# Who makes the weights' digits: moving casts, subtractions and loads between engines in a one-core layer kernel

## The chip, the core and the metric

The kernel runs on one core of a Trainium2 chip. The core has a matrix engine (TensorE, PE in the profile; its weight loads are PEld), a vector engine (VectorE, DVE), a scalar engine (ScalarE, ACT), a general engine (GpSimd, POOL) and a sync engine (SyncE, SP), which here only issues DMAs. Each engine works through its own instructions in order and waits at semaphores for the others. The metric is the device time of one execution in microseconds (us).

## The reference

One layer of an encoder in fp32, 1024 tokens by 1024 channels:

```python
h = rmsnorm(x, g_mix)
z = h @ w_in                               # pooling channels | q | k | v
y_pool = pool_mixer(z[..., :512], w_pool_grp, pool_scale)
y_attn = diff_attention(q, k, v, ...)      # 8 heads, two softmax maps each, chunk-causal
gates  = sigmoid(h @ w_gate + b_gate)      # 2 x 1024 columns
merged = gates[..., :1024] * (y_pool @ w_branch_pool) \
       + gates[..., 1024:] * (y_attn @ w_branch_attn)
x = x + merged @ w_out
h2 = rmsnorm(x, g_ffn)
x = x + square(relu(h2 @ w_up)) @ w_down
```

## The kernel before

**Digits.** A float32 operand is split into two digits in the matrix engine's fp32r form: hi is the rounded value, lo the rest. A product is three matmuls, hi·hi, hi·lo and lo·hi (`mm3`, L125 to L127). `split` makes the digits: the cast to hi on ACT (L119), the subtraction for lo on DVE, or on POOL where the caller says so (L120).

**Order.** A tile framework schedules the program: it takes instructions in the order in which they become ready in its own model of time, with a priority by program order, and adds the semaphores. `tc.issue_after(i)` lets what stands in the block come no sooner than instruction `i`. So a small edit can move instructions of every engine. After that, each engine's order is fixed.

**Stages** (times of the profile): until some 690 us the eight heads, each over eight tiles of queries: `z` (q, k, v of a tile), ACT's squares and DVE's `ms`, POOL's power (L236), DVE's `qn` (L429), POOL's scaling of `qn` (L435), transposes `tk` (to K and Q), scores `sc`, DVE's maxima `nm` (L490), ACT's exponentials `s` (L498), DVE's difference of the two maps (L507), transposes `ta` (to AT), `po`, and the head's norm (`oq`, `oqs`). Matmuls of the gates and the pooling groups (`g`, `u`, `yp`) fill in between; their weights `fwgate`, `fwpool` are split with lo on POOL, and a gate column half `go` (L733) is stored to `g_dram` by ACT's queue.

Within the heads `weight_unit` also prepares the digits for the attention branch. That branch multiplies by a seven-product scheme on 2 x 2 blocks (products "1" to "7"), so its weights are sums and differences of blocks of `w_branch_attn`. There are eight units. Each loads four blocks (`wq`), makes seven operands with four POOL operations (L767, L779) and calls `put` seven times: `put` splits 128x256 into the tile `wd` and stores it to `wa_dram` by SP (L764). `wd` has two buffers, so a put waits for the store of the one before the last. `PREP_AT` lists the `gate_step`s at which a unit is written.

Then the branches' start (690 to 757 us): `load_split` of the pooling branch's `ypT`, its weights `rbp` and `wbp`, the products `bp`, for each half `gate_half` (a load of `g`, L823, and ACT's sigmoid, L824), and `mp` = `bp` * `g` (L210). `load_a` (L869) issues the loads of the attention branch's digits, `wa`, from `wa_dram`; `y_scaled` and `split_b` make the other operand, `yb`. From 757 to 836 us follow the seven products `baX` and `baY` of 28 steps; behind each product `after(j)` adds it up (`plus`, L925), `gated` multiplies by the gate (L896) and adds `mp` (L897), and `merged` splits the result into `mT`. From 836 us on `op` multiplies `mT` by `w_out`, whose digits `wo` come from `ro` (`load_rows`, L159). Norm and MLP fill the rest.

Of the kernel before, what the change touches and what calls it, by code (L numbers as in the profile page):

```python
# [8 lines left out]
F32 = mybir.dt.float32  # L9
F32R = mybir.dt.float32r  # L10
I32 = mybir.dt.int32
AF = mybir.ActivationFunctionType
ALU = mybir.AluOpType
# [4 lines left out]
P = 128  # L18
S = 1024
# [3 lines left out]
H = 8  # L23
# [13 lines left out]
N_YU = 5  # L37
N_QKVW = 8 * H
N_AHEAD_B, N_AHEAD_A = 5, 3
PREP_AT = (3, 5, 6, 8, 9, 11, 12, 13)  # L40


START = "x0 g n0 w0 w1 w2u w3u x1 s0p s1 x2 s2p s3 x3"
# [14 lines left out]
def encoder_kernel(  # L58
# [21 lines left out]
    nc = tc.nc  # L80
    x, out = x[0], out[0]
    w_in, w_gate, w_out = w_in[0], w_gate[0], w_out[0]
    w_branch_pool, w_branch_attn = w_branch_pool[0], w_branch_attn[0]
# [6 lines left out]
    hp0 = [mix.enter_context(tc.tile_pool(name=f"hp0{i}", bufs=4)) for i in "ab"]  # L90
    hp1 = [mix.enter_context(tc.tile_pool(name=f"hp1{i}", bufs=4)) for i in "ab"]
# [11 lines left out]
    def htile(shape, dt, name, th):  # L103

        hcount[th] += 1
        return (hp1 if th else hp0)[(hcount[th] - 1) // 4 % 2].tile(shape, dt, tag="H", name=name)
# [4 lines left out]
    def raw(shape, name):  # L111
        return rpool.tile(shape, F32, tag="raw", name=name)

    def f(ap):
        return ap.bitcast(F32)

    def split(hi, lo, src, lo_eng=None):

        nc.scalar.copy(hi, src)  # L119
        (lo_eng or nc.vector).tensor_tensor(lo, src, f(hi), op=ALU.subtract)  # L120

    def mm3(ps, lhs_hi, lhs_lo, rhs_hi, rhs_lo, first, last, more=False):

# [15 lines left out]
    def fr_tile(shape, name):  # L139
        return fp.tile(shape, F32, tag="fr", name=name, bufs=N_FR)  # L140
# [15 lines left out]
    def load_rows(src, r0, c0, name, tile_fn):  # L156

        rw = raw([P, 2, 512], f"r{name}")
        nc.sync.dma_start(rw, src[r0 : r0 + 2 * P, c0 : c0 + 512].rearrange("(kk p) c -> p kk c", p=P))  # L159
        ws = []  # L160
        for j in range(2):
            w = tile_fn([P, 2, 512], f"w{name}_{j}")
            split(w[:, 0], w[:, 1], rw[:, j, :], nc.gpsimd)
            ws.append(w)
        return ws

# [17 lines left out]
    def load_split(src, r0, name, tile_fn):  # L184

        rw = raw([P, S], f"r{name}")
        nc.sync.dma_start(rw, src[r0 : r0 + P, :])
        return split_halves(rw, name, tile_fn)

    def y_scaled(d, rbs):  # L190
# [10 lines left out]
    def pair(t):  # L201
        return t[:, 0, :], t[:, 1, :]

    def branch_pool(d, ws, ps_fn):

        m = htile([P, S], F32, f"mp{d}", 1)
        gs_ = [gate_half(d, th) for th in range(2)]
        for th in range(2):
            ps = proj_T(ps_fn(f"bp{d}_{th}"), ws, lambda k, th: pair(ypT[k][th]), th, nk=4)
            nc.vector.tensor_tensor(m[:, th * 512 : (th + 1) * 512], ps, gs_[th], op=ALU.mult)  # L210
        mp.append(m)


    identf = units.tile([P, P], F32, name="identf")
# [9 lines left out]
    cols = const.tile([P, 24], F32, name="cols")  # L224
# [5 lines left out]
    g_dram = dram.tile([2 * D, S], F32, name="g_dram")  # L230
# [45 lines left out]
    with ExitStack() as ph:  # L276
# [356 lines left out]
        for g in range(-2, N + 8):  # L633
# [11 lines left out]
            for tok in ORDER:  # L645
                if tok not in gens:
                    i = g - tok[1]
# [7 lines left out]
    def fill_w(src, c0, name):  # L655
        ws = []
        for j in range(2):
            rw = fr_tile([P, 4, P], f"fr{name}_{j}")
            nc.sync.dma_start(
                rw, src[j * 512 : (j + 1) * 512, c0 : c0 + P].rearrange("(kk p) c -> p kk c", p=P)  # L660
            )
            w = fw_tile([P, 2, 4, P], f"fw{name}_{j}")
            split(w[:, 0], w[:, 1], rw, nc.gpsimd)
            ws.append(w)
        return ws

# [61 lines left out]
    def gate_cols(c):  # L728
        ws = fill_w(w_gate, c * P, f"gate{c}")
        for th in range(2):  # L730
            ps = fill_proj(ws, th, f"g{c}_{th}", spare_bank if c >= G_Z else fill_bank)
            fo = fo_tile(f"go{c}_{th}")
            stored["go"] = nc.scalar.activation(fo[:, 0:512], ps, AF.Identity, bias=cols[:, c : c + 1]).ins  # L733
            nc.scalar.dma_start(g_dram[c * P : (c + 1) * P, th * 512 : (th + 1) * 512], fo[:, 0:512])
            yield

# [5 lines left out]
            yield  # L742

    stored = {}
    wa_dram = dram.tile([28, P, 2, 512], F32, name="wa_dram")
    ORDER_BA = [(j, kk) for j in "1267543" for kk in range(4)]

    def weight_unit(src, digits, kk, ch):

        cs = slice(ch * 256, (ch + 1) * 256)  # L750
        q = fq.tile([P, 4, 256], F32, tag="mx", name=f"wq{kk}_{ch}")
        for i in range(2):
            r0 = (kk + 4 * i) * P
            nc.sync.dma_start(
                q[:, i::2, :], src[r0 : r0 + P, :].rearrange("p (i c) -> p i c", i=2)[:, :, cs]
            )
        a11, a12, a21, a22 = (q[:, i, :] for i in range(4))
        buf = fu_tile(f"wd{kk}_{ch}").rearrange("p (s h c) -> p s h c", s=2, h=2)

        def put(j, a):  # L760
            d = buf[:, nput[0] % 2]
            nput[0] += 1
            split(d[:, 0, :].bitcast(F32R), d[:, 1, :].bitcast(F32R), a, nc.gpsimd)
            nc.sync.dma_start(digits[ORDER_BA.index((j, kk))][:, :, cs], d)  # L764

        def minus(o, x_, y_):
            nc.gpsimd.tensor_tensor(o, x_, y_, op=ALU.subtract)  # L767

        nput = [0]
        put("1", a11)  # L770
        minus(a21, a11, a21)
        put("7", a21)
        put("2", a12)
        minus(a21, a22, a21)
        put("6", a21)
        put("4", a22)
        minus(a12, a12, a21)
        put("3", a12)
        nc.gpsimd.tensor_tensor(a11, a11, a21, op=ALU.add)  # L779
        put("5", a11)  # L780
# [3 lines left out]
    units_left = [(kk, ch) for kk in range(4) for ch in range(2)]  # L784

    def gate_step():
        more = next(gate_units, "end") != "end"
        steps[0] += 1
        if steps[0] in PREP_AT:
            with tc.issue_after(stored["go"]):  # L790
                weight_unit(w_branch_attn, wa_dram, *units_left.pop(0))
        return more

    for _ in range(G_FIRST):
        gate_step()
    for g in range(4):
        for _ in pool_group(g):
            gate_step()
    while gate_step():
        pass  # L800
    assert not units_left
# [18 lines left out]

    def gate_half(r0, th):
        gt = tmp(f"g{r0}_{th}")
        nc.sync.dma_start(gt, g_dram[r0 * P : (r0 + 1) * P, th * 512 : (th + 1) * 512])  # L823
        nc.scalar.activation(gt, gt, AF.Sigmoid, bias=zero)  # L824
        return gt

# [1 line left out]
        return [fu_tile(f"rb{d}")] if d in (0, 1, 2, 3, 5) else [tmp(f"rb{d}_{i}") for i in range(2)]  # L828

    ws_bp = {0: load_cols2(w_branch_pool, 0, "bp0", wt)}  # L830
    yr, wr, mp, mT = {}, {}, [], {}
    for d in range(NK - 2):
        yr[d] = y_scaled(d, row_factors(d))
    ypT = [load_split(p_dram, g * P, f"ypT{g}", ypt_tile) for g in range(4)]
# [31 lines left out]
    def load_a(n):  # L866

        wa_ba[n] = wa = (ut([P, 2, 512], F32R, f"wa{n}") if n < 8 or n > 23 else fw_tile([P, 2, 512], f"wa{n}"))
        nc.sync.dma_start(f(wa), wa_dram[n])  # L869
# [24 lines left out]
    def gated(d, th, c, src=None):  # L894

        nc.vector.tensor_tensor(c, src or c, gate_half(NK + d, th), op=ALU.mult)  # L896
        nc.gpsimd.tensor_tensor(c, c, mp[d][:, th * 512 : (th + 1) * 512], op=ALU.add)  # L897

    def merged(d, th, c):

        mT[d, th] = t = (hp1 if th else hp0)[d // 4].tile([P, 2, 512], F32R, tag="H", name=f"mT{d}_{th}")
        split(t[:, 0, :], t[:, 1, :], c)

    for d in range(NK):
        if d % 2 == 0 and d + 2 < NK:
            ws_bp[d + 2] = load_cols2(w_branch_pool, (d + 2) * P, f"bp{d + 2}", fw_tile)
        branch_pool(d, ws_bp[d - d % 2][d % 2], bank)
        if d == 1:
            for k in (6, 7):
                yr[k] = y_scaled(k, row_factors(k))  # L910
        load_a(d)
        if d > 2:
            split_b(d - 3)
    Yb = [bank(f"baY{dd}") for dd in range(4)]
    Xb = [bank(f"baX{dd}") for dd in range(4)]
    kept_ba = {}
# [11 lines left out]
    def after(j):  # L928

        if j == "1":  # L930
            copies("x1", Xb, [h_slab(f"x1_{i}") for i in range(2)])
        elif j == "2":
            for dd, c in plus("x1", Yb):
                gated(dd, 0, c)
                merged(dd, 0, c)
        elif j == "6":
            copies("U2", Xb, [up_slab(f"bU2_{i}") for i in range(2)])
        elif j == "7":
            copies("z7", Yb, [h_slab(f"z7_{i}") for i in range(2)])
        elif j == "5":  # L940
            for dd, c in plus("z7", Xb):
                gated(4 + dd, 1, c)
        elif j == "4":
            for dd, c in plus("U2", Yb):
                gated(4 + dd, 0, c)
                merged(4 + dd, 1, kept_ba["z7"][dd])
                merged(4 + dd, 0, c)
        else:
            for dd, c in enumerate(slabs([up_slab(f"c12_{i}") for i in range(2)])):
                gated(dd, 1, c, Xb[dd])  # L950
                merged(dd, 1, c)
# [492 lines left out]
```

## Time and profile before

| | |
|---|---|
| median of 3 runs | 1561.0 us (1560.26 to 1564.82) |
| the profiled execution | 1558.39 us, with a span of 1556.6 us |
| PE / DVE / ACT / POOL busy | 98% / 68% / 53% / 26% of the span |
| TensorE clock granted, mean | 0.999 |
| DMA | 235.81 MB, mean 151 GB/s |

All times of instructions come from one profiled execution. A row of a view names line, engine, operation and tiles (out<-in), with times in us and the mean of one instruction in ns; a row of waits names the engine and line that sat idle, and behind the arrow what released it. L12 is line 12 of the kernel before.

### The profile page before, as it was taken

The page shows a single profiled execution, that of the slowest core. Times are in us where ns is not written, and L with a number is a line of the kernel's source. Part 1 is how long each engine was busy: PE and PEld are TensorE (multiplying, and loading weights), DVE is VectorE, ACT ScalarE, POOL GpSimd, SP SyncE. Part 2 cuts the span into 40 slices and gives each one's busy share as a digit, 9 for nine tenths or more (in the row PEclk, how much of TensorE's full clock was granted, in tenths as well). Part 3 has the DMA queues.
Part 4 walks back from the last instruction along what each step waited for, and adds up shares of the span by engine and source line. Part 5 has one row for each costly group of instructions (what it writes and reads, how often), then busy time and mean ns, then how long its engine had stood idle before and what let it go on. Part 6 is the DMA issues. An engine that isn't in the chain of part 4 may idle for free.

```text
span 1556.6 us, 22409 instructions
## 1 busy us (share of the span) xinstructions
PE 1521.2 (98%) x7601; PEld 1310.7 (84%) x7601; DVE 1055.0 (68%) x2309; ACT 832.5 (53%) x1864; POOL 400.2 (26%) x520
## 2 busy tenths in 40 slices
PE   7999999999999999999999998999999999999999
PEld 6998988889998999877887887888888788888887
DVE  7777666687878787765569448776666568646662
ACT  6666566565656565554344556565555634333331
POOL 6446767451526252312037400000000000000000
PEclk9999999999999999999999999999999999999999
DMA  7133444220202021446576733545442689637750
GB/s 242 57 110 111 144 134 158 97 84 28 84 28 77 31 90 44 174 159 236 169 269 196 227 111 114 178 165 185 137 143 108 236 312 391 209 122 236 240 193 27
DMA packets 183277, 235.81 MB, mean 151 GB/s; under 512 B 11685, under 2 KB 114810, under 8 KB 183162
## 3 DMA queue, kind: packets, MB, share of 16 engines
q1 hardware_dynamic: 165754, 207.08, 40.0%
q10 hardware_dynamic: 17408, 27.30, 4.7%
q8 instruction: 60, 0.98, 0.3%
q14 instruction: 55, 0.45, 0.1%
HBM read 165.10 MB, written 69.24 MB: 151 GB/s over the span
## 4 chain that ended last, share of the span: by engine, by line
PE 47%; DMA 2%; DVE 2%; issue 2%; ACT 1%; POOL 1%; SPq 0%; POOLq 0%; ACTq 0%; DVEq 0%
PE Da L125 4%; PE Da L127 4%; PE Da L126 4%; PE Db L125 3%; PE Db L127 3%; PE Db L126 3%; PE X L125 2%; PE X L127 2%; PE X L126 2%; PE Z L127 2%; PE Z L126 2%; PE Z L125 2%; PE op L127 2%; PE op L125 1%; PE op L126 1%
## 5 line engine op out<-in xcount | busy, mean ns | idle before, releaser
L125 PE MATMUL z<-wqkv,hT 128*128 128x384 f32 x512 | 174.3, 340 | 1.4 <-DVE qn L429 1.4
L126 PE MATMUL z<-wqkv,hT 128*128 128x384 f32 x512 | 173.4, 339 | 0.5 <-POOL wqkv L120 0.5
L127 PE MATMUL z<-wqkv,hT 128*128 128x384 f32 x512 | 173.3, 339 | 0.0
L498 ACT ACTIVATE s<-s,nm 128x256 f32<-128x256 f32 (+7 forms) x128 | 99.6, 779 | 62.8 <-DVE nm L490 59.7
L125 PE MATMUL g<-hT,fwgate 128*128 128x512 f32 x256 | 101.0, 394 | 0.2 <-ACT go L733 0.2
L125 PEld LDWEIGHTS z<-wqkv,hT 128*128 128x128 f32 x512 | 96.5, 188 | 5.0 <-DVE qn L429 2.1
L127 PE MATMUL g<-hT,fwgate 128*128 128x512 f32 x256 | 100.7, 394 | 0.0
L126 PE MATMUL g<-hT,fwgate 128*128 128x512 f32 x256 | 100.6, 393 | 0.0
L126 PEld LDWEIGHTS z<-wqkv,hT 128*128 128x128 f32 x512 | 96.5, 188 | 4.0 <-POOL wqkv L120 1.0
L127 PEld LDWEIGHTS z<-wqkv,hT 128*128 128x128 f32 x512 | 96.4, 188 | 2.4 <-DVE hT L120 0.5
L236 POOL TENSOR_TENSOR ms<-ms,mhalf 128x4 f32<-128x4 f32 x64 | 67.1, 1049 | 102.5 <-DVE ms L235 86.0
L490 DVE CUSTOM_DVE_ANT_0 s<-sc,dist 128x512 f32<-128x512 f32 (+3 forms) x128 | 74.9, 586 | 11.9 <-PE sc L488 10.1
L120 POOL TENSOR_TENSOR wqkv<-rqkv,wqkv 128x384 fp32r<-128x384 f32 x60 | 63.8, 1082 | 22.2 <-ACT wqkv L119 19.0
L120 DVE TENSOR_TENSOR AS<-s,AS 128x512 fp32r<-128x512 f32 x64 | 43.8, 689 | 37.9 <-ACT AS L119 37.8
L487 PE MATMUL sc<-K,Q 128*128 128x512 f32 (+2 forms) x192 | 66.6, 358 | 0.5 <-DVE nm L490 0.4
L488 PE MATMUL sc<-K,Q 128*128 128x512 f32 (+2 forms) x192 | 65.9, 357 | 0.0
L458 ACT CAST Q<-tk 64x128 fp32r<-64x128 f32 x128 | 33.0, 258 | 51.2 <-DVE K L457 50.1
L457 DVE TENSOR_TENSOR K<-tk,K 64x128 fp32r<-64x128 f32 x128 | 37.0, 289 | 34.2 <-ACT K L456 31.0
L435 POOL TENSOR_TENSOR qn<-qn,ggh 128x128 f32<-128x128 f32 x64 | 32.2, 503 | 101.5 <-DVE qn L429 93.8
L461 ACT CAST Q<-tk 64x128 fp32r<-64x128 f32 x128 | 33.2, 260 | 42.3 <-DVE Q L460 40.7
L125 PEld LDWEIGHTS g<-hT,fwgate 128*128 128x128 f32 x256 | 48.1, 188 | 8.4 <-ACT go L733 0.5
L127 PEld LDWEIGHTS g<-hT,fwgate 128*128 128x128 f32 x256 | 48.1, 188 | 8.3
(460 smaller groups left out, 4740.9 us busy)
## 6 DMA issues: line engine op xcount, KB each, us to landing
wd<-in_w_down_dram SPq DMA_DIRECT2D x56, 512.0 KB, 5.4
wu<-in_w_up_dram SPq DMA_DIRECT2D x32, 512.0 KB, 4.5
udS<-us SPq DMA_DIRECT2D x64, 256.0 KB, 2.5
ur<-udS SPq DMA_DIRECT2D x32, 512.0 KB, 3.3
wa_dram<-wd SPq DMA_DIRECT2D x56, 256.0 KB, 2.4
wa<-wa_dram SPq DMA_DIRECT2D x28, 512.0 KB, 6.0
rqkv<-in_w_in_dram SPq DMA_DIRECT2D x64, 192.0 KB, 2.7
ud<-u ACTq DMA_DIRECT2D x48, 256.0 KB, 2.3
```

Of the source, the lines that this page charges most:

```text
L120: (lo_eng or nc.vector).tensor_tensor(lo, src, f(hi), op=ALU.subtract)
L125: nc.tensor.matmul(ps, lhs_hi, rhs_hi, start=first, stop=False, **kw)
L126: nc.tensor.matmul(ps, lhs_hi, rhs_lo, start=False, stop=False, **kw)
L127: nc.tensor.matmul(ps, lhs_lo, rhs_hi, start=False, stop=last, **kw)
L236: nc.gpsimd.tensor_tensor(dst, dst, mhalf[:, :n], op=ALU.pow)
L457: nc.vector.tensor_tensor(K[other, m, c0 : c0 + P], k, f(k_hi), op=ALU.subtract)
L458: nc.scalar.copy(q_hi, q)
L461: nc.scalar.copy(Q[other, m, 1, :], q)
L487: nc.tensor.matmul(dst, Q[:, i, 0, :], rhs, start=True, stop=False)
L488: nc.tensor.matmul(dst, Q[:, i, 1, :], rhs, start=False, stop=True)
L490: nc.vector.tensor_tensor_reduce(out=s[i][:, c : c + w], in0=sc[:, 0:w], in1=dist[:, o0 + c : o0 + c + w], scale=2.0 ** -(h + 1), scalar=B ...
L498: nc.scalar.activation(s[i][:, 0:n], s[i][:, 0:n], AF.Exp, bias=last, scale=-1.0, accum_out=Z[:, i, t : t + 1])
```

## The change

Five things change.

1. `put` takes the cast to hi from ACT to POOL (L762 of the changed kernel); lo stays on POOL (L763).
2. `PREP_AT` has five steps in place of eight, and the other three units are written after the pooling groups 0, 1 and 2. A unit is ordered behind the last lo subtraction of `fwgate` or `fwpool`, no longer behind the last `go`.
3. `load_a(d)` is ordered behind the load of a gate half: that of `g0` for d below 4, that of `g` d − 1 from there on.
4. `mp` is no tile of 1024 columns any more but two halves, in pool tiles of hp1 that two neighbouring d share; `z7` is turned into `mT` at product "5" and not at "4".
5. The gated add (L897 before, L904 after) and the lo subtractions of `wo` are on DVE, no longer on POOL.

```diff
-PREP_AT = (3, 5, 6, 8, 9, 11, 12, 13)
+PREP_AT = (3, 5, 7, 9, 12)
...
-            split(w[:, 0], w[:, 1], rw[:, j, :], nc.gpsimd)
+            split(w[:, 0], w[:, 1], rw[:, j, :])
...
-        m = htile([P, S], F32, f"mp{d}", 1)
...
-            nc.vector.tensor_tensor(m[:, th * 512 : (th + 1) * 512], ps, gs_[th], op=ALU.mult)
-        mp.append(m)
+            nc.vector.tensor_tensor(mp[d, th], ps, gs_[th], op=ALU.mult)
...
-            split(w[:, 0], w[:, 1], rw, nc.gpsimd)
+            stored["lo"] = split(w[:, 0], w[:, 1], rw, nc.gpsimd).ins
...
-            stored["go"] = nc.scalar.activation(fo[:, 0:512], ps, AF.Identity, bias=cols[:, c : c + 1]).ins
+            nc.scalar.activation(fo[:, 0:512], ps, AF.Identity, bias=cols[:, c : c + 1])
...
-            split(d[:, 0, :].bitcast(F32R), d[:, 1, :].bitcast(F32R), a, nc.gpsimd)
+            nc.gpsimd.tensor_copy(d[:, 0, :].bitcast(F32R), a)
+            nc.gpsimd.tensor_tensor(d[:, 1, :].bitcast(F32R), a, d[:, 0, :], op=ALU.subtract)
...
         if steps[0] in PREP_AT:
-            with tc.issue_after(stored["go"]):
-                weight_unit(w_branch_attn, wa_dram, *units_left.pop(0))
+            prepare_weights()
         return more
+
+    def prepare_weights():
+        with tc.issue_after(stored["lo"]):
+            weight_unit(w_branch_attn, wa_dram, *units_left.pop(0))
...
         for _ in pool_group(g):
             gate_step()
+        if g < 3:
+            prepare_weights()
...
-        nc.gpsimd.tensor_tensor(c, c, mp[d][:, th * 512 : (th + 1) * 512], op=ALU.add)
+        nc.vector.tensor_tensor(c, c, mp[d, th], op=ALU.add)
...
+    for i, (a_, th) in enumerate(((0, 0), (2, 0), (4, 1), (6, 1), (4, 0), (6, 0), (0, 1), (2, 1))):
+        t = hp1[i // 4].tile([P, 2, 512], F32, tag="H", name=f"mp{a_}_{th}")
+        mp[a_, th], mp[a_ + 1, th] = t[:, 0, :], t[:, 1, :]
...
-        load_a(d)
+        with tc.issue_after(loaded["g0_1" if d < 4 else f"g{d - 1}_1"]):
+            load_a(d)
...
             for dd, c in plus("z7", Xb):
                 gated(4 + dd, 1, c)
+                merged(4 + dd, 1, c)
         elif j == "4":
             for dd, c in plus("U2", Yb):
                 gated(4 + dd, 0, c)
-                merged(4 + dd, 1, kept_ba["z7"][dd])
                 merged(4 + dd, 0, c)
```

Three places show how the instructions' order moves. The first is POOL in the second head. `ms` and `qn` belong to the query tiles, `wd` and `wq` to a weight unit. Before:

```order
L236 TENSOR_TENSOR ms_4_1541<-ms_4_1541,mhalf 128x4
L120 TENSOR_TENSOR wd_1_7339<-wq_1_7336,wd_1_7339 128x256 x2
L767 TENSOR_TENSOR wq_1_7336<-wq_1_7336 128x256
L779 TENSOR_TENSOR wq_1_7336<-wq_1_7336 128x256
L120 TENSOR_TENSOR wd_1_7339<-wq_1_7336,wd_1_7339 128x256 x2
L767 TENSOR_TENSOR wq_1_7336<-wq_1_7336 128x256
```

In the changed kernel the same engine, in the first head (L234 and L433 there are L236 and L435 here, L762 is the cast, L763 the subtraction):

```order
L762 CAST wd_0_7244<-wq_0_7241 128x256
L234 TENSOR_TENSOR ms_4_719<-ms_4_719,mhalf 128x4
L762 CAST wd_0_7244<-wq_0_7241 128x256
L763 TENSOR_TENSOR wd_0_7244<-wq_0_7241,wd_0_7244 128x256
L433 TENSOR_TENSOR qn_3_651<-qn_3_651,ggh_364 128x128
L120 TENSOR_TENSOR fwgate_0_7300<-frgate_0_7298,fwgate_0_7300 128x512
L763 TENSOR_TENSOR wd_0_7244<-wq_0_7241,wd_0_7244 128x256
L767 TENSOR_TENSOR wq_0_7241<-wq_0_7241 128x256
L762 CAST wd_0_7244<-wq_0_7241 128x256
```

Two operations for each put now stand in POOL's queue between the `ms` and `qn` of the tiles, and the units begin a head earlier; in order, five of them stand in the first part of the heads and three in later heads.

The second place is SP's queue at the branches' start, where `g` is a gate half, `wa` a step's digits, `rypT` and `rbp` the pooling branch's operands. Before:

```order
L823 DMA g_0_8978<-g_dram 128x512
L869 DMA wa_8975<-wa_dram 128x1024
L869 DMA wa_9028<-wa_dram 128x1024
L869 DMA wa_9073<-wa_dram 128x1024
L823 DMA g_1_8981<-g_dram 128x512
L869 DMA wa_9110<-wa_dram 128x1024
L187 DMA rypT_8916<-p_dram 128x1024
L187 DMA rypT_8924<-p_dram 128x1024
L869 DMA wa_9158<-wa_dram 128x1024
L148 DMA rbp_8932<-in_w_branch_pool_dram 128x4x256
```

The changed kernel's SP queue from the same load on (L828 is the gate half there, L876 the digits):

```order
L828 DMA g_0_8984<-g_dram 128x512
L828 DMA g_1_8987<-g_dram 128x512
L187 DMA rypT_8916<-p_dram 128x1024
L187 DMA rypT_8924<-p_dram 128x1024
L148 DMA rbp_8940<-in_w_branch_pool_dram 128x4x256
L148 DMA rbp_9036<-in_w_branch_pool_dram 128x4x256
L828 DMA g_0_8948<-g_dram 128x512
L148 DMA rbp_9119<-in_w_branch_pool_dram 128x4x256
L159 DMA ro_0_9945<-in_w_out_dram 128x2x512
L828 DMA g_1_8951<-g_dram 128x512
L876 DMA wa_8982<-wa_dram 128x1024
```

The first load of `wa` now stands behind two gate halves of each of the first columns, the pooling branch's operands and a load of `w_out`.

The third place is DVE at the end of the products, where `bU` holds half the merged result, `c` the last quarter, and `mT` takes the split. Before:

```order
L120 TENSOR_TENSOR mT_0_9794<-bU_0_9545,mT_0_9794 128x512
L120 TENSOR_TENSOR mT_1_9802<-z_0_9619,mT_1_9802 128x512
L120 TENSOR_TENSOR mT_0_9805<-bU_0_9545,mT_0_9805 128x512
L120 TENSOR_TENSOR mT_1_9813<-z_1_9620,mT_1_9813 128x512
L896 TENSOR_TENSOR c_0_9880<-baX_9292,g_1_9882 128x512
L120 TENSOR_TENSOR mT_0_9816<-bU_1_9546,mT_0_9816 128x512
```

The changed kernel's DVE there (L903 is the gate's product, L904 the add that was POOL's, `wo` a split of `w_out`):

```order
L904 TENSOR_TENSOR bU_0_9545<-bU_0_9545,mp_0_8936 128x512 x2
L904 TENSOR_TENSOR bU_1_9546<-bU_1_9546,mp_0_8937 128x512 x2
L903 TENSOR_TENSOR c_0_9880<-baX_9292,g_1_9882 128x512
L120 TENSOR_TENSOR wo_6_0_10103<-ro_6_10101,wo_6_0_10103 128x512
L120 TENSOR_TENSOR wo_6_1_10106<-ro_6_10101,wo_6_1_10106 128x512
L903 TENSOR_TENSOR c_0_9880<-baX_9293,g_1_9890 128x512
L120 TENSOR_TENSOR mT_0_9803<-bU_0_9545,mT_0_9803 128x512
```

The adds and two subtractions of `wo` now stand ahead of the first `mT` from `bU`, and the splits of `z` have moved up, out of this stretch. On PE the first `op` tile that needs this `mT` (`op_0_9979` with `wo_4`) comes after 12 matmuls before, and after 19 in the changed kernel, since a second token tile's matmuls stand in between.

More of the change, by code (lines that the diff above doesn't have):

```diff
@@ L119, in split @@
         nc.scalar.copy(hi, src)
-        (lo_eng or nc.vector).tensor_tensor(lo, src, f(hi), op=ALU.subtract)
+        return (lo_eng or nc.vector).tensor_tensor(lo, src, f(hi), op=ALU.subtract)
     def mm3(ps, lhs_hi, lhs_lo, rhs_hi, rhs_lo, first, last, more=False):
@@ L186, in load_split @@
         rw = raw([P, S], f"r{name}")
-        nc.sync.dma_start(rw, src[r0 : r0 + P, :])
+        loaded[name] = nc.sync.dma_start(rw, src[r0 : r0 + P, :]).ins
         return split_halves(rw, name, tile_fn)
@@ L744, in encoder_kernel @@
     stored = {}
+    loaded = {}
     wa_dram = dram.tile([28, P, 2, 512], F32, name="wa_dram")
@@ L822, in gate_half @@
         gt = tmp(f"g{r0}_{th}")
-        nc.sync.dma_start(gt, g_dram[r0 * P : (r0 + 1) * P, th * 512 : (th + 1) * 512])
+        loaded[f"g{r0}_{th}"] = nc.sync.dma_start(
+            gt, g_dram[r0 * P : (r0 + 1) * P, th * 512 : (th + 1) * 512]
+        ).ins
         nc.scalar.activation(gt, gt, AF.Sigmoid, bias=zero)
@@ L830, in encoder_kernel @@
     ws_bp = {0: load_cols2(w_branch_pool, 0, "bp0", wt)}
-    yr, wr, mp, mT = {}, {}, [], {}
+    yr, mp, mT = {}, {}, {}
     for d in range(NK - 2):
@@ L896, in gated @@
         nc.vector.tensor_tensor(c, src or c, gate_half(NK + d, th), op=ALU.mult)
-        nc.gpsimd.tensor_tensor(c, c, mp[d][:, th * 512 : (th + 1) * 512], op=ALU.add)
+        nc.vector.tensor_tensor(c, c, mp[d, th], op=ALU.add)
     def merged(d, th, c):
-        mT[d, th] = t = (hp1 if th else hp0)[d // 4].tile([P, 2, 512], F32R, tag="H", name=f"mT{d}_{th}")
+        mT[d, th] = t = (hp1[1 - d // 4] if th else hp0[d // 4]).tile([P, 2, 512], F32R, tag="H", name=f"mT{d}_{th}")
         split(t[:, 0, :], t[:, 1, :], c)
+    for i, (a_, th) in enumerate(((0, 0), (2, 0), (4, 1), (6, 1), (4, 0), (6, 0), (0, 1), (2, 1))):
+        t = hp1[i // 4].tile([P, 2, 512], F32, tag="H", name=f"mp{a_}_{th}")
+        mp[a_, th], mp[a_ + 1, th] = t[:, 0, :], t[:, 1, :]
     for d in range(NK):
```

## The prediction

> **What bounds the kernel now.** I read the page's totals first, then what TensorE waits for, then the busy time by stretch.
>
> ```profile
> span 1556.6 us, 22409 instructions
> PE 1521.2 (98%) x7601; PEld 1310.7 (84%) x7601; DVE 1055.0 (68%) x2309; ACT 832.5 (53%) x1864; POOL 400.2 (26%) x520
> ```
>
> TensorE (PE) is busy 98% of the span. The change leaves its matmuls as they are, so it can win only from the remaining 1556.6 − 1521.2 = 35.4 us, and can lose without a limit. Next comes the list of what PE waited for (total, times, longest).
>
> ```profile
> PE hps L262 <- DVE hn L257: 9.5, 2, 8.7
> PE ta L543 <- DVE s L507: 2.7, 1, 2.7
> PE op L127 <- DVE mT L120: 1.7, 2, 0.9
> PE bp L125 <- DVE mp L210: 1.5, 1, 1.5
> PE z L125 <- DVE qn L429: 1.4, 2, 1.0
> PE tk L447 <- ACT Q L461: 1.2, 1, 1.2
> PE po L579 <- DVE oqs L120: 0.9, 1, 0.9
> PE u L125 <- ACT go L733: 0.7, 1, 0.7
> PE po L126 <- DVE AT_4l L120: 0.5, 1, 0.5
> PE op L125 <- ACT mT L119: 0.5, 1, 0.5
> PE z L126 <- POOL wqkv L120: 0.5, 1, 0.5
> PE sc L487 <- DVE nm L490: 0.4, 1, 0.4
> ```
>
> The first row is the start, which the change does not touch. I sort the others by stage. In the heads, ACT or DVE was late in ta 2.7, tk 1.2, u 0.7 and sc 0.4, together 5.0 us; POOL stands behind z 1.4 (qn needs ms from POOL) and z 0.5, together 1.9. At the branch start there are bp 1.5, oqs 0.9 and AT_4l 0.5, together 2.9. At the merge there are op 1.7 and 0.5, together 2.2. All that the change can reach is therefore 12.0 us.
>
> Busy time by stretch (columns: stretch, its length, PE, PEld, DVE, ACT, POOL, then clock, DMA share, GB/s) shows how much room the other engines have:
>
> ```profile
> 100.00:200.00 100.00, 99.50 (x581) 91.57 (x579) 70.39 (x227) 62.71 (x184) 57.45 (x78) 1.00 0.35 114
> 200.00:300.00 100.00, 94.92 (x547) 85.81 (x545) 67.82 (x223) 62.95 (x186) 63.15 (x87) 1.00 0.43 138
> 300.00:400.00 100.00, 97.75 (x564) 89.76 (x563) 79.24 (x254) 64.15 (x191) 41.62 (x59) 1.00 0.18 56
> 780.00:840.00 60.00, 60.00 (x265) 49.13 (x264) 46.89 (x50) 33.33 (x58) 35.07 (x23) 1.00 0.70 237
> 840.00:920.00 80.00, 77.87 (x361) 63.81 (x360) 41.16 (x60) 32.96 (x62) 28.22 (x24) 1.00 0.62 201
> ```
>
> **Part 1, digits by POOL and spread.** The tile wd tells what the 56 puts cost, and who waited for whom:
>
> ```profile
> L119 ACT CAST wd<-wq x56: 391/407/428, 81.4 to 300.7; 128x256 fp32r<-128x256 f32 x56
> L120 POOL TENSOR_TENSOR wd<-wq,wd x56: 723/739/1255, 81.9 to 301.2; 128x256 fp32r<-128x256 f32 x56
>   ACT wd L119: 30.8, 20
>   DMA wa_dram<-wd: 28.1, 25
> ```
>
> ACT waited 28.1 us for a store to free the double buffer, with softmax work of the heads queued behind it; POOL waited 30.8 us for ACT's cast. One such wait can be followed on ACT at the stall of tk:
>
> ```profile
> 273.66 0.40 ACT L119 CAST wd<-wq 128x256 fp32r<-128x256 f32 x1 [1.07 <-DMA wa_dram<-wd]
> 273.97 0.26 ACT L461 CAST Q<-tk 64x128 fp32r<-64x128 f32 x1
> ```
>
> The cast of Q (L461), for which tk waited 1.2 us, stood behind a cast of wd that waited 1.07 us for a store. After the change both the casts and this wait leave ACT: 56 × 0.407 = 22.8 us of work and 28.1 of waiting. I credit the whole 5.0 us that ACT and DVE lost in the heads (from 0, if other work is the cause, to 5.0): that is 5.0/28.1 = 0.18 us of PE per us of wait.
>
> POOL takes 56 casts of 128x256. No row shows this cast on POOL; the nearest are these:
>
> ```profile
> L767 POOL TENSOR_TENSOR wq<-wq 128x256 f32<-128x256 f32 x24 | 19.3, 803 | 18.4 <-DMA wq<-in_w_branch_attn_dram 18.0
> L706 POOL COPY sum<-u 128x1 f32<-128x1 f32 x8 | 2.2, 280 | 3.7 <-ACT u L698 2.3 <-DMA g_dram<-go 1.3
> wa_dram<-wd SPq DMA_DIRECT2D x56, 256.0 KB, 2.4
> ```
>
> The floor is 0.28 us (a copy of one column), the top 0.80 (a subtraction of the same tile). I take 0.76, the mean of the wd subtraction (42.0 us by 56 is 0.75; same tile, same output form): 56 × 0.76 = 42.6 us, between 15.7 and 45. The Trainium skill ("GPSIMD Engine Reference", 4.1 Engine selection) calls an elementwise op of one input roughly line-rate on GpSimd and a two-input one about twice as slow; a cast by that estimate would be near 0.4 us and the casts near 23, which no row here shows, and my sum goes by the 42.6.
>
> What does it do to the queue behind it? POOL's ms (L236) and qn (L435) are passed on to DVE and so to z and tk. Over the 222 us of wd, POOL was busy about 0.60 and blocked by ACT's cast for 30.8/222 = 0.14, so occupied for 0.74. After the change this block is gone, the casts add 42.6/222 = 0.19 to 0.60, and the store wait comes to POOL. The store takes 2.4 us and a put on POOL 0.76 + 0.75 = 1.5, with other POOL work in between; I estimate half of the 28.1, 14 us or 0.06. That makes 0.85. Units 1 to 5 stay in the first 230 us by the order, so I take this dense case; three later units go to stretches where POOL has 58 of 100 us free. Waits grow like r/(1 − r), from 2.85 to 5.7, so the 1.9 us of POOL's lateness doubles: +1.9 (0 if spread work stays hidden; if nothing is hidden, (42.6 + 28.1) × 0.18 = +12.7). Heads: −5.0 + 1.9 = **−3.1**.
>
> A rule that speaks against it stands beside these rows, DVE's scaled subtractions in the heads:
>
> ```profile
> L507 DVE SCALAR_TENSOR_TENSOR s<-s,cf,s x32: 870/1152/1725, 84.5 to 696.6; 128x640 f32<-128x640 f32 x8, 128x768 f32<-128x768 f32 x8, 128x896 f32<-128x896 f32 x8, 128x1024 f32<-128x1024 f32 x8
> L120 DVE TENSOR_TENSOR oqs<-oq,oqs 128x256 fp32r<-128x256 f32 x32 | 18.2, 570 | 6.4 <-ACT oqs L119 5.8
> ```
>
> By the Trainium skill ("SBUF — State Buffer", section "SBUF: two separate sides"), a GpSimd operation that reads SBUF and a DVE operation with two SBUF inputs lock each other out for a whole instruction. The spread of 870 to 1725 ns over these shapes neither shows nor excludes it. By that rule casts would hold up (32 × 1.15 + 18.2)/700 = 8% of DVE's time against 42.6 us, 3.4 us on DVE, some 0.6 on PE: 1555 in place of my time. My sum leaves it out.
>
> **Parts 3 and 4, the branch start.** The chain of waits runs here through a gate column's store and its load, before sigmoid and product mp. The rows behind it give what such transfers usually take, what SP issued, and the first product:
>
> ```profile
> 710.87 7.68 DMA g_dram<-go
> 718.57 3.60 DMA g<-g_dram
> g_dram<-go ACTq DMA_DIRECT2D x32, 256.0 KB, 2.5
> wa<-wa_dram SPq DMA_DIRECT2D x28, 512.0 KB, 6.0
> 709.94 1.41 SPq L869 DMA_DIRECT2D wa<-wa_dram  x3
> L125 PE MATMUL baX<-yb,wa x64: 387/389/499, 759.3 to 835.4; 128*128 128x512 f32 x64
> ```
>
> The store took 7.68 us where 2.5 is usual, and three loads of wa had been issued on SP 0.9 us before it. With load_a behind the gate loads, these wa loads leave SP's queue here and this store meets less traffic: bp's 1.5 goes, and of the other 1.4 I take 0.5 (AT and oqs belong to the last head's tail on ACT and DVE). **−2.0**, between −2.9 and +6.0, one landing of a wa load, if the first product then waits for it; that product starts at 759.3, 37 us after this load of g lands, so I take no loss. The two-half mp tiles and the earlier mT of z7 issue the same operations: nothing.
>
> **Part 5, the merge.** POOL gives up 24 subtractions of wo and 16 gated adds; DVE takes 40 operations of 128x512 with two SBUF inputs. Prices:
>
> ```profile
> L897 POOL TENSOR_TENSOR bU<-bU,mp x4: 1739/1741/1748, 827.3 to 837.5; 128x512 f32<-128x512 f32 x4
> 836.31 1.77 DVE L120 TENSOR_TENSOR mT<-bU,mT 128x512 fp32r<-128x512 f32 x1
> L120 DVE TENSOR_TENSOR AS<-s,AS 128x512 fp32r<-128x512 f32 x64 | 43.8, 689 | 37.9 <-ACT AS L119 37.8
> ```
>
> DVE pays 0.69 us for such a subtraction where POOL has nothing to do, and 1.77 for the same size while POOL works: 40 × 0.69 = 27.5 us more work between 780 and 920, where DVE was busy 46.89 + 41.16 of 140. It fits in the 52 us free, and the stretched ones shrink besides. An add of 1.74 on POOL becomes 0.69 on DVE in the chain bU, mT, op; PE meanwhile does 19 op matmuls on mT 0 to 3 before the first on mT 4. So the 1.7 us of op behind DVE goes; the 0.5 behind ACT's mT stays: **−1.7**, between −2.2 and +1.5. The loss would come from wo's last subtractions, which now stand in DVE's queue ahead of mT and wait for their load of ro.
>
> **Sum.** −3.1 − 2.0 − 1.7 = −6.8. The profiled execution took 1558.4 us, of which the span is 1556.6; it becomes 1551.6. The median of the runs shown, 1561.0, is 2.6 above it; so 1554.2, said as 1554.
>
> **Rivals.** *Slower, by the store wait on POOL.* Every put waits 2.4 − 1.5 = 0.9 us for its buffer, 56 × 0.9 = 50 us, with ms and qn queued behind it, and POOL's 42.6 + 50 = 93 us cost PE the same 0.18 each: +16.7. With −5.0, −2.0 and −1.7 that is +8.0: 1569. It decides from POOL's cost of 5.0 + 3.7 + 4.7 = 13.4 us on (74 us of lateness). For it: POOL's 63.15 of 100. Against it: wgate and ms work between the puts gives the store time.
>
> *Same, the wait only changes engine.* What ACT gives, POOL takes: heads 0, and −3.7 remains: 1557.3. For it: the heads' chain goes round through all engines, DVE at 70 to 79 of 100 among them.
>
> *More: every listed wait goes,* −12.0: 1549.0. For it: POOL no longer waits for ACT at all. Against it: ends of waits are seldom given back whole, the next engine in the heads' chain is late instead.
>
> **How the numbers follow.** About 0.3% (4.7 us) is what a measurement of this kernel can tell from no change: faster is below 1556.3, slower above 1565.7. Forecast 0.48, same 0.27, more 0.12, slower 0.13. From the forecast's spread (heads −5 to 0) some 0.04 falls in "same". So faster 0.56, same 0.31, slower 0.13. The range reaches from the rival that gains more to the edge of the slower one, 1548 to 1565; the forecast's own is 1551 to 1558.
>
> **What the profile after would show.** Right: no wait for the store on ACT, casts of wd on POOL near 0.76 us or below; rows ta, tk and u gone from PE's waits; the go store near 710 at 2.5 to 4 us, bp's row gone; mT on DVE near 0.69 and op's row under 0.5. Wrong: new rows z behind qn or tk behind POOL of more than 5 us between 50 and 230, POOL at 90 of 100 there; baX waiting for wa at 760; op waiting for mT behind ro.

## The result, and the profile after

The changed kernel takes 1556.0 us (median of 9 runs, 1551.5 to 1558.3) against 1560.3 for the kernel before: a ratio of 0.9966, with a 95% interval of 0.9953 to 0.9979, some 5 us less. The profiled execution is the quickest of the nine, 1551.45 us with a granted clock of 1.000; in the other eight the clock was 0.996 to 0.999 and the span 1552 to 1557 us. Its span is 7.1 us shorter than that of before, so about 2 us of this belong to the execution and not to the change. I read places from the traces, and sizes from the ratios.

The page's totals after:

```profile
span 1549.5 us, 22331 instructions
PE 1519.3 (98%) x7601; PEld 1309.8 (85%) x7601; DVE 1052.1 (68%) x2349; ACT 814.5 (53%) x1808; POOL 361.0 (23%) x536
```

POOL does less than before, although it took 56 casts over: it gave away 40 longer operations. What PE waited for (total, times, longest):

```profile
PE hps L260 <- DVE hn L255: 8.8, 1, 8.8
PE ta L541 <- DVE AT_4l L120: 2.0, 2, 1.6
PE X L125 <- ACT U L1213: 2.0, 1, 2.0
PE sc L485 <- DVE nm L488: 1.9, 4, 0.7
PE Z L125 <- ACT BT1h L119: 1.5, 1, 1.5
PE ta L541 <- DVE ms L233: 1.4, 1, 1.4
PE ta L541 <- ACT Q L459: 1.2, 1, 1.2
...
PE z L125 <- DVE qn L427: 0.7, 1, 0.7
```

The rows of bp, po and op are gone. In the heads ta no longer waits for `s`, nor u for `go`, but others of the same size came: ta behind AT_4l, `ms` and Q, and sc behind `nm` grew from 0.4 to 1.9 us. Busy time by stretch says when (columns as before: PE, PEld, DVE, ACT, POOL, clock, DMA share, GB/s):

```profile
100.00:200.00 100.00, 99.91 (x586) 92.50 (x585) 75.91 (x249) 59.89 (x174) 57.65 (x87) 1.00 0.32 104
200.00:300.00 100.00, 99.69 (x590) 92.51 (x589) 71.42 (x241) 59.91 (x179) 42.01 (x64) 1.00 0.20 67
400.00:500.00 100.00, 96.26 (x555) 87.42 (x554) 76.44 (x250) 59.48 (x174) 49.73 (x76) 1.00 0.24 79
600.00:700.00 100.00, 96.75 (x512) 82.57 (x511) 65.32 (x182) 50.35 (x134) 25.45 (x34) 1.00 0.37 126
700.00:780.00 80.00, 80.00 (x355) 66.12 (x355) 38.20 (x61) 33.97 (x56) 9.80 (x8) 1.00 0.68 232
840.00:920.00 80.00, 80.00 (x378) 66.38 (x378) 43.81 (x74) 34.40 (x66) 3.80 (x7) 1.00 0.60 198
```

Between 200 and 300 us PE's idle time fell from 5.1 us to 0.3; between 400 and 700 it grew. Over the whole heads nothing was won. The same view for the first 700 us in one row, first of before, then of after:

```profile
0.00:700.00 700.00, 679.54 (x3869) 617.85 (x3870) 519.21 (x1614) 432.14 (x1237) 324.50 (x464) 1.00 0.32 103
```

```profile
0.00:700.00 700.00, 679.04 (x3871) 616.13 (x3872) 519.33 (x1623) 412.79 (x1182) 345.27 (x520) 1.00 0.31 99
```

Idle 20.5 us before, 21.0 after. The branch start (700 to 780) went from 2.3 to 0, the end of the merge (840 to 920) from 2.1 to 0. These 4.4 us make up most of what the changed kernel won: PE's idle time over the whole span fell from 35.4 to 30.2 us. The question is what became of the heads' gain.

### The profile page after: what moved, and what is told of

It reads as the page before. It is cut to its first block, busy times and chain, and to the rows that moved or that the text cites. A ratio compares the mean times of both kernels' runs of the same rounds, so it can differ in the third digit from the quotient of the medians.

```text
span 1549.5 us, 22331 instructions
## 1 busy us (share of the span) xinstructions
PE 1519.3 (98%) x7601; PEld 1309.8 (85%) x7601; DVE 1052.1 (68%) x2349; ACT 814.5 (53%) x1808; POOL 361.0 (23%) x536
## 4 chain that ended last, share of the span: by engine, by line
PE 84%; DVE 6%; DMA 3%; issue 3%; ACT 2%; SPq 1%; POOL 0%; POOLq 0%; ACTq 0%; DVEq 0%
PE z L125 5%; PE z L127 5%; PE z L126 5%; PE Da L126 4%; PE Da L127 4%; PE Da L125 4%; PE g L125 3%; PE g L126 3%; PE g L127 3%; PE Db L126 3%; PE Db L127 3%; PE Db L125 3%; PE X L125 2%; PE X L127 2%; PE X L126 2%
## 5 line engine op out<-in xcount | busy, mean ns | idle before, releaser
L234 POOL TENSOR_TENSOR ms<-ms,mhalf 128x4 f32<-128x4 f32 x64 | 67.0, 1046 | 96.2 <-DVE ms L233 79.4
L488 DVE CUSTOM_DVE_ANT_0 s<-sc,dist 128x512 f32<-128x512 f32 (+3 forms) x128 | 74.6, 584 | 17.6 <-PE sc L486 16.1
L120 DVE TENSOR_TENSOR AS<-s,AS 128x512 fp32r<-128x512 f32 x64 | 43.8, 687 | 35.5 <-ACT AS L119 35.3
L120 POOL TENSOR_TENSOR fwgate<-frgate,fwgate 128x512 fp32r<-128x512 f32 x32 | 43.4, 1361 | 87.4 <-ACT fwgate L119 78.8
L125 PEld LDWEIGHTS g<-hT,fwgate 128*128 128x128 f32 x256 | 48.1, 188 | 9.9 <-ACT go L731 1.1
L127 PEld LDWEIGHTS g<-hT,fwgate 128*128 128x128 f32 x256 | 48.0, 188 | 8.7
L126 PEld LDWEIGHTS g<-hT,fwgate 128*128 128x128 f32 x256 | 48.1, 188 | 8.0
```

The lines of the kernel that those rows point to most:

```text
L120: return (lo_eng or nc.vector).tensor_tensor(lo, src, f(hi), op=ALU.subtract)
L125: nc.tensor.matmul(ps, lhs_hi, rhs_hi, start=first, stop=False, **kw)
L126: nc.tensor.matmul(ps, lhs_hi, rhs_lo, start=False, stop=False, **kw)
L127: nc.tensor.matmul(ps, lhs_lo, rhs_hi, start=False, stop=last, **kw)
L234: nc.gpsimd.tensor_tensor(dst, dst, mhalf[:, :n], op=ALU.pow)
L488: nc.vector.tensor_tensor_reduce(out=s[i][:, c : c + w], in0=sc[:, 0:w], in1=dist[:, o0 + c : o0 + c + w], scale=2.0 ** -(h + 1), scalar=B ...
```

## The experiments

All ratios are against the kernel before, run on the same chip. "Idle" is PE's idle time in a stretch, its length less PE's busy time.

| run | 0 to 700 | 700 to 780 | 780 to 920 | ratio (95%) |
|---|---|---|---|---|
| before | 20.5 | 2.3 | 2.1 | 1 |
| changed kernel | 21.0 | 0 | 0 | 0.9966 (0.9953 to 0.9979) |
| part 1 alone | 15.0 | 0.9 | 2.4 | 0.9966 (0.9953 to 0.9979) |
| part 5 alone | 19.5 | 1.0 | 0.3 | 0.9977 (0.9967 to 0.9987) |
| parts 1 and 5 | 15.5 | 1.7 | 0 | 0.9927 (0.9913 to 0.9942) |
| changed, without 3 | 20.9 | 0 | 0 | 0.9982 (0.9971 to 0.9994) |
| changed, without 5 | 21.4 | 0 | 4.6 | 1.0021 (1.0009 to 1.0033) |
| changed, without 1 | 24.2 | 1.2 | 0 | 1.0044 (1.0028 to 1.0059) |
| changed, without 2 | 16.2 | 1.5 | 0 | 0.9916 (0.9902 to 0.9930) |
| changed, without 2 and 3 | 16.9 | 2.0 | 0 | 0.9929 (0.9917 to 0.9941) |
| one late unit | 18.0 | 2.3 | 0 | 0.9969 (0.9957 to 0.9981) |
| late units, no POOL work | 19.4 | 0.4 | 0 | 0.9963 (0.9950 to 0.9975) |
| late units, four copies | 13.8 | 0 | 0 | 0.9908 (0.9886 to 0.9930) |

**Part 1 alone**, in the kernel before:

```diff
-            split(d[:, 0, :].bitcast(F32R), d[:, 1, :].bitcast(F32R), a, nc.gpsimd)
+            nc.gpsimd.tensor_copy(d[:, 0, :].bitcast(F32R), a)
+            nc.gpsimd.tensor_tensor(d[:, 1, :].bitcast(F32R), a, d[:, 0, :], op=ALU.subtract)
```

> The kernel before with part 1 alone: POOL makes the hi digits of wd, the units stay where they were (82 to 301 us in the trace of before). Theory A (the trace of after: PE's idle time in the first 700 us was 20.5 us before and 21.0 after, so the heads gave nothing): taking the casts off ACT removes the idle time between 100 and 300 us (5.6 us before), and new waits of ta, sc or tk come up elsewhere in the heads; the span changes by less than 2 us, ratio 0.999 to 1.001. Theory B (the prediction's): the 5.0 us of the heads are won and POOL gives back 1.9: -3 us, ratio 0.998. Rival C (the store wait on POOL holds up ms and qn): z and tk wait over 5 us more, +8 us, ratio 1.005. In all of them a cast of 128x256 on POOL takes about 0.40 us, as after.

Theory A fell: the heads' idle time went down by 5.4 us and stayed down. B was nearer, with one difference: POOL gave nothing back. The row of the first 700 us, and the tile wd with what its engine waited for:

```profile
0.00:700.00 700.00, 684.96 (x3906) 625.77 (x3907) 527.05 (x1624) 420.01 (x1188) 344.14 (x520) 1.00 0.33 106
```

```profile
L763 POOL CAST wd<-wq x56: 389/397/933, 43.6 to 264.0; 128x256 fp32r<-128x256 f32 x56
L764 POOL TENSOR_TENSOR wd<-wq,wd x56: 728/738/1569, 44.7 to 265.9; 128x256 fp32r<-128x256 f32 x56
...
  DMA wa_dram<-wd: 8.7, 9
```

A cast takes 397 ns, and POOL waits 8.7 us for stores where ACT had waited 28.1. A few waits of PE under 1.5 us are left in the heads (g, sc, ta, trr); none is behind qn. The one behind POOL, trr for the head's norm (1.4 us, after 600 us), comes more than 330 us after the last cast. The merge keeps its 2.4 us, since part 5 is not in it.

**Part 5 alone**, in the kernel before: the subtractions of wo and the gated adds on DVE.

```diff
-            split(w[:, 0], w[:, 1], rw[:, j, :], nc.gpsimd)
+            split(w[:, 0], w[:, 1], rw[:, j, :])
...
-        nc.gpsimd.tensor_tensor(c, c, mp[d][:, th * 512 : (th + 1) * 512], op=ALU.add)
+        nc.vector.tensor_tensor(c, c, mp[d][:, th * 512 : (th + 1) * 512], op=ALU.add)
```

> The kernel before with part 5 alone: gated adds and wo's subtractions on DVE, mp still a tile of 1024 columns and z7 merged at product 4. Theory A (the merge won 2.1 us by DVE no longer being stretched beside POOL): PE's idle time in 840 to 920 us falls from 2.1 to under 0.6, DVE's subtraction mT from bU goes from 1.63 to 0.69 us, span -1.5 to -2.1, ratio about 0.999. Rival D (it was the earlier mT of z7, part 4, that won it): op still waits 1 us or more for mT, ratio 1.000.

Theory A held, D fell: without the earlier mT of z7 the wait of op is gone as well. The gain by the ratio, 0.0023 or 3.6 us, is more than the 0.001 that A named.

**The changed kernel without part 5**, the same edit the other way round:

```diff
-            split(w[:, 0], w[:, 1], rw[:, j, :])
+            split(w[:, 0], w[:, 1], rw[:, j, :], nc.gpsimd)
...
-        nc.vector.tensor_tensor(c, c, mp[d, th], op=ALU.add)
+        nc.gpsimd.tensor_tensor(c, c, mp[d, th], op=ALU.add)
```

> The changed kernel without part 5: gated adds and wo's subtractions on POOL again, mT of z7 still made at product 5. Theory A: DVE's subtractions of 128x512 in 800 to 860 us go back to 1.2 to 1.8 us, op waits 1.5 to 2.5 us again; ratio to the kernel before about 0.998. Rival D (part 4's earlier mT of z7 is what took the wait away): op has no wait over 0.3 us, ratio 0.9966.

Theory A held in direction; the cost, 0.0055 or 8.6 us, is four times what I had expected. The subtractions of mT from bU in this run, and in the run with part 5 alone (min/median/max in ns):

```profile
L120 DVE TENSOR_TENSOR mT<-bU,mT x4: 674/1364/1776, 838.4 to 846.7; 128x512 fp32r<-128x512 f32 x4
```

```profile
L120 DVE TENSOR_TENSOR mT<-bU,mT x4: 682/684/684, 833.1 to 843.3; 128x512 fp32r<-128x512 f32 x4
```

PE idles 4.6 us between 840 and 920, more than before the change, and 5.1 us more over the whole span (35.3 against 30.2). The rest goes with PE's busy time: 1525.8 us against 1519.3, with a granted clock of 0.91 or 0.92 in four stretches of 20 us (from 20, 400, 640 and 880 on). Part of this gap is that the changed kernel's profile is its quickest execution; over all runs the mean clock is 0.995 here and 0.998 there.

**The changed kernel without part 3**:

```diff
-        with tc.issue_after(loaded["g0_1" if d < 4 else f"g{d - 1}_1"]):
-            load_a(d)
+        load_a(d)
```

> The changed kernel without part 3: load_a is not ordered behind the gates' loads; 7251 of 7257 PE instructions keep their order. Theory A: wa loads come back ahead of the gate store and load near 710 us, that store takes 5 us or more again in place of what it takes after, bp waits 1 to 2.3 us, and 700 to 780 us loses that much: +1.5 to +2.3, ratio to the kernel before about 0.9975 where after had 0.9966. Rival E (the branch start was won by the last head's tail, AT and oqs, being hidden behind 110 gate matmuls that now come later): PE stays without idle time in 700 to 780, ratio 0.9966.

The time went as A said (+0.0016), the trace as E said: PE has no idle time in 700 to 780 without part 3 either. The two speak against each other, and the intervals of the two kernels overlap. PE's idle time over the whole span is the same in the two profiles, 30.2 us; what differs is its busy time (1523.8 against 1519.3) and the clock (0.996 against 1.000). So a worth of part 3 by itself is not shown. In both, 133 gate matmuls are left behind the last ta, in place of 45, and may cover the branch start. That their number decides it is not shown, and two runs below speak against it: with 132 of them PE idled 2.3 us there, with 83 not at all.

**The changed kernel without part 2**, units at the old steps:

```diff
-PREP_AT = (3, 5, 7, 9, 12)
+PREP_AT = (3, 5, 6, 8, 9, 11, 12, 13)
...
-        if g < 3:
-            prepare_weights()
...
-            with tc.issue_after(stored["lo"]):
+            with tc.issue_after(stored["go"]):
...
-            nc.scalar.activation(fo[:, 0:512], ps, AF.Identity, bias=cols[:, c : c + 1])
+            stored["go"] = nc.scalar.activation(fo[:, 0:512], ps, AF.Identity, bias=cols[:, c : c + 1]).ins
```

> The changed kernel without part 2: units at the eight old steps, ordered behind go, POOL's casts kept. In the order of its instructions 69 gate matmuls are left behind the last ta, against 133 in the changed kernel and 45 in the kernel before. Theory F (part 1 won 5 us in the heads, as part 1 alone showed, and the spreading of part 2 took it back by moving 64 gate matmuls, 14.6 us of filling work, out of the heads): PE's idle time in the first 700 us is 15 us in place of 21, the merge stays without idle time; span 1544 to 1547, ratio 0.993 to 0.9945. Theory G (what part 1 alone won is chance of one order, and the changed kernel's late stalls have nothing to do with part 2): idle 20 to 21 us, ratio 0.9966.

Theory F held: idle 16.2 us in the heads, and the ratio, 0.9916, is better than F said. At 1546.9 us (5 runs) it is the quickest complete version of this study, 0.5% under the changed kernel; it has parts 1, 3, 4 and 5.

```profile
0.00:700.00 700.00, 683.76 (x3900) 625.17 (x3901) 523.88 (x1622) 418.21 (x1186) 345.20 (x520) 1.00 0.31 101
```

**The same, also without part 3** (the edit shown above):

> The last kernel also without part 3 (load_a not ordered behind the gates' loads): only 69 gate matmuls to cover the branch start, and wa loads ahead of the gate loads. Theory A (part 3 is worth its 1.5 to 2.3 us where the cover is short): idle time of 1 to 2 us in 700 to 780, ratio 0.001 to 0.0015 above the last kernel's. Theory E (gate matmuls behind the last ta cover it): within 0.0007 of the last kernel's.

The difference is 0.0013, as A said; the intervals overlap again.

**Parts 1 and 5 in the kernel before**, both edits shown above:

> The kernel before with parts 1 and 5 only. If the parts add (part 1 alone 0.9966, part 5 alone 0.9977): ratio 0.9943, with idle time 15 us in the first 700 us and none in 840 to 920. If part 4 matters (the earlier mT of z7), op still waits for mT by about 1 us: 0.995.

0.9927: they add, and a little more. The changed kernel without 2 and 3 differs from this one by part 4 only, and is at 0.9929: part 4 is worth nothing that shows.

**The changed kernel without part 1**, the cast on ACT again:

> The changed kernel without part 1: ACT makes the hi digits again, the units stay spread; 121 gate matmuls are left behind the last ta. Theory F (the filling work that is missing in the heads costs 6 us, and ACT's wait for the store costs another 3 to 5): idle time in the first 700 us of 24 to 27 us, ratio 0.999 to 1.001. Rival H (spreading by itself takes away ACT's waits, so part 1 adds nothing): idle time 21 us or less, ratio 0.9966 as the changed kernel.

The idle time came out as F said (24.2 us), the time was worse than either: 1.0044. Rival H fell: ACT still waited 16.1 us for stores of wd, beside 28.1 before. In the changed kernel part 1 is worth 0.0078, 12 us. Idle time in the table is 4.4 us of that; the rest goes with PE's busy time, 1533.1 us in this profile against 1519.3, and a clock of 0.89 to 0.94 in seven stretches of 20 us.

**What in the spreading costs?** Three kernels changed the late units of the changed kernel. The first has one of them in place of three:

```diff
-PREP_AT = (3, 5, 7, 9, 12)
+PREP_AT = (3, 5, 6, 7, 9, 10, 12)
...
-        if g < 3:
+        if g == 1:
             prepare_weights()
```

> The changed kernel with one late unit in place of three: seven units at steps 3, 5, 6, 7, 9, 10 and 12, one behind pooling group 1. In the order 132 gate matmuls are still left behind the last ta, as in the changed kernel (133). Theory F (what costs is the filling work that leaves the heads): idle time in the first 700 us 20 to 22 us as in the changed kernel, ratio 0.996 to 0.997. Theory P (what costs is POOL's work beside DVE in the later heads, 19 us less in two of three places): about a third of the 5 to 6 us, idle 16.5 to 18 us, ratio 0.993 to 0.994.

The time is that of the changed kernel, as F said; idle time in the heads, 18.0, is at the edge of what P said, and 2.3 us more idle stand behind them, where bp waited 1.2 us for a gate column (`go`) and baX 1.0 us for `mp`. The trace shows how a late unit keeps the filling work out. PE's time on gate matmuls around the unit (its POOL work runs from 465 to 492), in stretches of 20 us (busy PE, count, clock, DMA share, GB/s):

```profile
440.00:460.00 20.00, 6.23 (x24) 1.00 0.11 37
460.00:480.00 20.00, 0.00 (x0) 1.00 0.55 166
480.00:500.00 20.00, 0.00 (x0) 0.91 0.21 72
500.00:520.00 20.00, 6.37 (x24) 1.00 0.18 58
```

And the timeline there, on PE, POOL, ACT, and PE again:

```profile
474.42 0.39 PE L127 MATMUL u<-hT,fwpool 128*128 128x512 f32 x1
```

```profile
491.46 0.73 POOL L763 TENSOR_TENSOR wd<-wq,wd 128x256 fp32r<-128x256 f32 x1
```

```profile
495.14 0.59 ACT L696 COPY u<-u 128x512 f32<-128x512 f32 x1
```

```profile
501.43 0.39 PE L125 MATMUL g<-hT,fwgate 128*128 128x512 f32 x1
```

The product u of the next pooling group was done at 474.8. Its copy out of PSUM came 20 us later: the tile it goes to (`fu_tile`, one buffer) is the tile wd of the unit, and the last of its seven stores was issued after 491.46 + 0.73. The filling work has one PSUM bank, so no filler could run in between, and PE idled 1.7 us from 480 to 500. In the changed kernel the first late unit does the same: u ends at 388.9, its copy follows at 412.7. One of these copies names the store in the trace; without part 2 the first copy of that group comes at 392.16, 1 us behind its product:

```profile
412.70 0.61 ACT L696 COPY u<-u 128x512 f32<-128x512 f32 x1
585.05 0.59 ACT L696 COPY u<-u 128x512 f32<-128x512 f32 x1 [0.53 <-DMA wa_dram<-wd]
```

```profile
392.16 0.56 ACT L696 COPY u<-u 128x512 f32<-128x512 f32 x1
```

The second kernel leaves the late units without POOL operations, and the third with four copies:

```diff
         def put(j, a):
+            if late:
+                nc.sync.dma_start(digits[ORDER_BA.index((j, kk))][:, :, cs], q[:, 0:2, :])
+                return
```

> The changed kernel with the three late units left without any POOL operation: they load their blocks and store the blocks themselves seven times, with no sums, casts or subtractions (that part of the result is left out). 132 gate matmuls are left behind the last ta. Theory F: idle time in the first 700 us 19 to 22 us, ratio 0.996 to 0.997. Theory P: 15 to 17 us, ratio 0.992 to 0.994.

```diff
+        if late:
+            for i in range(4):
+                nc.gpsimd.tensor_copy(buf[:, i // 2, i % 2], q[:, i])
...
         def put(j, a):
+            if late:
+                nc.sync.dma_start(digits[ORDER_BA.index((j, kk))][:, :, cs], buf[:, nput[0] % 2])
+                nput[0] += 1
+                return
```

> The changed kernel with the three late units left with four POOL copies each, which fill the tile wd once; then seven stores of it (the sums, casts and subtractions of these units are left out). 83 gate matmuls are left behind the last ta. Theory F: idle time in the first 700 us 15.5 to 18 us, ratio 0.993 to 0.9945. Theory P: as the run without POOL operations, 15 to 17 us, ratio 0.992 to 0.994. Only the two runs together tell them apart.

Theory P fell. Without any POOL work in the late units the kernel is as slow as the changed one (0.9963); with a little POOL work and the filler back, it is at 0.9908, better than both theories said. What goes with the time is the filling work. PE's time on gate matmuls between 300 and 640 us (its busy time and their count come first), in order: the changed kernel; without part 2; no POOL work; four copies.

```profile
300.00:640.00 340.00, 52.92 (x201) 1.00 0.26 86
```

```profile
300.00:640.00 340.00, 59.80 (x233) 0.99 0.20 64
```

```profile
300.00:640.00 340.00, 52.75 (x208) 0.99 0.26 87
```

```profile
300.00:640.00 340.00, 60.39 (x236) 1.00 0.28 90
```

The kernel without POOL work does not use the tile fu in its late units; it holds `mx`, which the pooling group's `mix` shares, from its loads to its last store. The one with four copies frees mx after the copies and holds fu. So either tile can do it if it is held long; how the loss divides between the two in the changed kernel stays open.

## Why the prediction was right, and where it was not

Forecast −6.8 us; the ratio of the runs says −5.3 (−3.3 to −7.3). The sum came out near, by two errors that nearly cancel, and that is luck. Without part 2 the change is worth 13.1 us by the ratio (0.9916), 6.3 more than I forecast for the whole; part 2, which I had costed at nothing, took 7.8 back. For the heads I forecast −3.1, and their idle time went up by 0.5.

- *ACT freed of casts and store waits, −5.0 in the heads:* right. Part 1 alone took 5.4 us of idle time out of the heads, most of it between 200 and 300 us where the waits had been. My ceiling was too low, though: the list of waits in the prediction leaves out three larger rows of the heads that the same view has, ta behind AT_0l (1.2 us), ta behind Q (0.7) and yp behind go (0.6). By the same counting, "all that the change can reach" is 14.5 us and not 12.0.
- *POOL's lateness, +1.9:* mis-sized, nothing of it shows in part 1 alone. The cast takes 0.40 us and not 0.76, 22 us in all and not 42.6, and the store wait on POOL is 8.7 to 10.4 us and not 14. The estimate of near 0.4 us, from what the Trainium skill says of one-input operations ("GPSIMD Engine Reference", 4.1 Engine selection), was a better price than the nearest row, a subtraction with two inputs. The slow rival's 0.9 us of waiting for each put did not come: 8.7 us of it in 56 puts.
- *The units' new places, costed at nothing:* the step that failed. I looked at POOL's free time in the later heads (58 of 100 us) and not at what a unit holds: the tiles fu and mx, which the pooling groups need. Part 2 costs 0.0050, 7.8 us (0.9916 against 0.9966). Of this the profiles show 4.8 us of idle time in the heads, less 1.5 at the branch start; where the rest lies stays open. The gate matmuls that it drove out of the heads stand in the order of the instructions (133 behind the last ta, 45 before), and no term counts them. Part 1 alone already leaves 69 there, so 64 of the 88 come with part 2. Their number is the same in all, but in the heads a filler covers a wait, and behind them there is only a short start to cover.
- *Branch start, −2.0:* right in size (2.3 to 0), but the cause that I named is not needed: PE has no idle time there without the new order of loads either. What took its place stays open; the gate matmuls that come later are the likely cover, but the run with 132 of them behind the last ta idled 2.3 us. What part 3 is worth by itself, 0.0013 to 0.0016 in two pairs, lies within the intervals; the go store's longest landing fell with it, from 6.4 to 3.7 us in the one pair and from 4.3 to 3.3 in the other.
- *Merge, −1.7:* right (2.1 to 0) and by the step named: mT from bU takes 0.685 us at the median after the change, and no load of ro held it up:

```profile
L120 DVE TENSOR_TENSOR mT<-bU,mT x4: 682/685/687, 836.6 to 839.6; 128x512 fp32r<-128x512 f32 x4
```

- *The rivals:* "same" described the heads well (nothing won there), for another reason than a wait that changes engine.
- *The lock between POOL and DVE,* set aside in the sum: it exists here, as the last section shows, but the casts did not make the heads slower: with them on POOL the heads lost 5.4 us of idle time.

## What to carry to other kernels

When a block of side work is moved, list what it holds (tiles, PSUM banks, queue places) and who else uses the same buffer, before looking at how busy its engine is there. Filling work is worth most where a chain has gaps: count how much of it an edit moves out of such a stretch, since a constant total hides it. A change in five parts should be measured part by part: here four parts brought 0.84%, and the other one, part 2, took 0.50 of it back.

## What the runs showed of the hardware

POOL and DVE hold each other up, as the Trainium skill states ("SBUF — State Buffer", section "SBUF: two separate sides"), and it reached further than I had weighed, which was DVE operations with two SBUF inputs. The section also names DVE operations in a two-port mode; whether the one below runs in such a mode, no run here shows. In the changed kernel a DVE operation of 128x4 with one input, 0.17 us at the median, lasted 1.03 us and ended with POOL's subtraction of a gate weight, having begun 0.43 us after it:

```profile
434.97 1.03 DVE L233 TENSOR_SCALAR ms<-ms 128x4 f32<-128x4 f32 x1
435.91 0.55 DVE L120 TENSOR_TENSOR AT_4l<-ta,AT_4h 128x384 fp32r<-128x384 f32 x1
```

```profile
434.54 1.43 POOL L120 TENSOR_TENSOR fwgate<-frgate,fwgate 128x512 fp32r<-128x512 f32 x1 [9.71 <-ACT fwgate L119]
```

Of the 64 operations of this kind 48 took at most 0.17 us. The other 16 took 0.22 to 1.20 us, and each of them ended 0.02 to 0.03 us after a POOL operation that had begun before it. So a POOL operation of 1.4 us can cost DVE most of its length. In the other direction a cast on POOL in the same kernel took 1.17 us in place of 0.40, beside a DVE operation on the two softmax maps (L505) that had begun 0.11 us before it and took 1.02 us. Behind the one shown stands AT_4l, for which ta waited 1.6 us, the longest wait of the heads after the change; how much of that wait is due to the lock was not tested.

The granted clock fell below 1.00 for a few microseconds in places where PE had idled. In the run with one late unit it was 0.91 from 480 to 500 us; PE idled 1.7 us between 485 and 490, and the clock was 0.70 from 490 to 495 and 1.00 again behind that. Not every wait does this: the changed kernel's own profile idles 2.1 us between 420 and 440 at a clock of 1.00. The executions of one kernel scatter by some 0.4% (the nine spans of the changed kernel go from 1549.5 to 1556.5), which is as much as the change is worth, and only in part with the clock: 1549.5 at 1.000, 1554.0 to 1556.5 at 0.996, but also 1554.6 at 0.999.
